# Experts' rows added to the residual in DRAM, in a two-layer decoder trunk

## The chip, the cores and the metric

One core of one Trainium2 chip runs the whole program. The metric is the device time of one execution in microseconds (us).

## The reference

Two layers work on x of 512 tokens by 1024. Each has a token mixer (RWKV-7 in the first, attention with a forget gate in the second), a layer norm, a mixture of 16 experts of which each token takes two, and another layer norm. The part that matters here, for each layer:

```
h   = layer_norm(ALPHA * h + mixed, ln_g[i, 0], ln_b[i, 0])
ffn = sum over the token's two experts of  gate * (silu(h @ w_gate) * (h @ w_up)) @ w_down
h   = layer_norm(ALPHA * h + ffn, ln_g[i, 1], ln_b[i, 1])      # LN_EPS 1e-5, ALPHA = sqrt(2)
```

The gates of a token's two experts are scores divided by their sum. With these inputs the experts of the first layer get, in the order in which the kernel takes them, 167, 82, 19, 59, 131, 65, 53, 4, 145, 53, 50, 6, 89, 62, 26 and 13 rows (1,024 in all); the second layer's counts differ by at most 9.

## The kernel before

Matmuls keep fp32 precision by splitting each operand in a high and a low part (`split`: ACT copies, DVE subtracts) and summing three products (`mm3`). The weights of an expert are six halves of 1 MB; SP loads them into a ring of eight buffers (`load`, `place`), and a buffer's next load is issued as soon as its half is split.

`After.norm` ends the first norm of a layer: tile i (128 tokens) is written to `hd` in DRAM, by POOL's queue, and by SP's for the last tile. `moe` then ranks the tokens, writes a table of slots to DRAM with scatters (L426) and reads it back as `TB`: for each expert's rows the token (`src`), a place in `yd` (`dst`: the token's row in the first or second 512 rows) and the gate.

The loop over experts (last lines of `moe`) issues, in this order: `more(e)`, which runs only where an expert has more than 128 rows (3 experts a layer) and scatters up to 64 rows of a second block; the gather of the first 128 rows of expert e+2 into `xg` (L251); `gather2(e+1)`, the rows past 128 of expert e+1 in halves, into `xo` (L259; it runs for every expert); and `expert(e)`. That multiplies, transposes the next expert's `xg` and, late, its `xo` (`xposeB`, L305), and ends with the scatter of 128 rows of `y` into `yd` (L334). Rows past an expert's count have an index out of range and are dropped. Scatters, gathers and their waits stand in order on POOL's queue. The scatters are declared independent of each other, since each slot of `yd` is written once. `rest` (over 192 rows) does not run with these inputs.

`Combine` adds the parts and takes the second norm. `load_h` brings h from `hd` during the last experts; `load_y` loads, after the last scatter, the two halves of `yd` for each of four tiles (eight loads of 512 KB on SP). The letter in `how` says who adds: D is DVE alone, V is PE with ALPHA h and one part and DVE with the other, P is PE alone, G is POOL and DVE. The layer norm follows (`ln_steps`), whose four passes with g and b go to DVE or POOL, whichever a planner (`Threads`) expects to be free sooner. In the first layer this stands at the head of `fox`: each normed tile is transposed and split, and the value projection (`t_values`, 24 matmuls per tile and half) starts on it; `FX_SCHED` holds the planner's start times of the four tiles (`TK`) and of the value weights (`TV`). In the second layer it ends the program, and each tile is stored.

Of the kernel before, what the change touches and what calls it, by code (L numbers as in the profile page):

```python
# [118 lines left out]

def ln_stats(C, z, n):  # L120
# [4 lines left out]
    nc.vector.tensor_scalar(sm[:,14:15],sm[:,13:14],LN_EPS,None,op0=ALU.add)  # L125
    nc.scalar.activation(sm[:,15:16],sm[:,14:15],AF.Sqrt)
# [50 lines left out]

def moe(C, L, W, hd, load, tail, late=()):

# [3 lines left out]
    with ExitStack() as ctx:  # L183
        p1=ctx.enter_context(tc.tile_pool(name=f"m{L}p1",bufs=1)); wk=ctx.enter_context(tc.tile_pool(name=f"m{L}k",bufs=1))
        fx=lambda n,shape,dt=F32: wk.tile(shape,dt,name=n,bufs=1)
        yd=C.dram.tile([1024,D],F32,name=f"yd{L}"); tab=C.dram.tile([8192,4],I32,name=f"tab{L}")
        TB=p1.tile([128,64,4],I32,name="TB"); TB2=p1.tile([128,64,4],I32,name="TB2")
# [84 lines left out]
        def slot(m): return his[m%NH],los[m%NH]  # L272
        src=lambda e,b=0: TB[:,4*e+b,0:1]; dst=lambda e,b=0: TB[:,4*e+b,1:2]; gate=lambda e,b=0: TB[:,4*e+b,2:3].bitcast(F32); gate2=lambda e,b=0: TB2[:,4*e+b,2:3].bitcast(F32)
        def xposeT(xg,hf,bk):
# [54 lines left out]
        def outB(n,y):  # L329
            t=(xo,su)[n][0:64]; p=(pgo,py[0])[n]  # L330
            nc.scalar.activation(t,p[64:128],AF.Copy); V.tensor_tensor(y[0:64,n*512:(n+1)*512],t,p[0:64],op=ALU.add)
        scat=[]
        def scatter(ix,y,n):
            st=nc.gpsimd.indirect_dma_start(out=yd[:,:],out_offset=bass.IndirectOffsetOnAxis(ap=ix[0:n],axis=0),  # L334
                in_=y[0:n],in_offset=None,bounds_check=2*T-1,oob_is_err=False)
            for o in scat: tc.declare_no_dep(st.ins,o.ins,reason="rows of other slots")
            scat.append(st)
        def more(e):

            y=ys[1-e%2 if e else 0]; w=[slot(6*e+j) for j in range(6)]; f2=gate2(e,1) if e else g0[:,1:2]  # L340
            with tc.If(rs[e]>128):
                guB(w[0],0); guB(w[1],1); nc.scalar.activation(xo,pgo,AF.Copy)
                if e==0: gates0(1)
                guB(w[2],2); upB(0,f2)
                guB(w[3],3); upB(1,f2); hidBT(0); hidBS(0); hidBT(1); hidBS(1)
                for n in range(2): dnB(w[4],4,n)
                for n in range(2): dnB(w[5],5,n); outB(n,y)
                scatter(dst(e,1),y,64)


        def expert(e):
# [16 lines left out]
            if next_: xposeB()  # L368
            lo(4); dnA(w[5],5,1); outA(1,y,fo); scatter(dst(e),y,128); hi(5); lo(5)
        def again(e,j):  # L370
            r=raws[6+j%2]; w=slot(6*e+j); place(r,L,W,6*e+j,nc.gpsimd); split(C,*w,r); return w
        def rest(e,blk):

            f=gate(e,blk); ix=dst(e,blk)
            if blk==1: V.memset(i2[0:64],int(BIG)); V.tensor_copy(i2[64:128],ix[64:128]); ix=i2
# [33 lines left out]
        V.tensor_reduce(red[:,1,:,None],ct(mt),axis=AX.X,op=ALU.add)  # L409
        V.tensor_tensor(red[:,2,0:4],red[:,1,0:4],red[:,1,4:8],op=ALU.add); V.reciprocal(red[:,2,0:4],red[:,2,0:4])  # L410
        V.tensor_tensor(C.rec[:,:,2].rearrange("p (c t) -> p c t",c=2).bitcast(F32),red[:,1].rearrange("p (c t) -> p c t",c=2),red[:,2:3,0:4].to_broadcast([128,2,NT]),op=ALU.mult)
# [33 lines left out]
        for e in range(NE):  # L445
# [4 lines left out]
            expert(e)  # L450
    return yd

class Combine:


    def __init__(s, C, hd, g, b):
        s.C,s.hd,s.g,s.b=C,hd,g,b; s.how='PPPP'
        s.h=[part(C.raws[4+i//2],i%2) for i in range(NT)]; s.y0=[part(C.raws[6+i//2],i%2) for i in range(NT)]
        s.gb,s.bb=part(C.raws[2],0),part(C.raws[2],1)
# [9 lines left out]
    def spread2(s):  # L469
        C=s.C  # L470
        for n in range(4): C.nc.scalar.activation(C.raws[2][:,n*512:(n+1)*512],C.bk[4+n],AF.Copy)
    def load_h(s, j):
        s.C.nc.sync.dma_start(s.C.raws[4+j].rearrange("p (i n) -> p i n",i=2),s.hd[j*256:(j+1)*256,:].rearrange("(i p) n -> p i n",p=128))
    def load_y(s, yd, y1, late):

        nc=s.C.nc; d=nc.sync.dma_start; s.y1=y1
        for i in range(NT):
            d(s.y0[i],yd[i*128:(i+1)*128,:]); d(y1[i],yd[T+i*128:T+(i+1)*128,:])
        if late: s.spread(); s.spread2()
        pe=[i for i in range(NT) if s.how[i] in 'PV']  # L480
        for i in pe: nc.scalar.activation(s.h[i],s.h[i],AF.Copy,scale=ALPHA); s.add(i,s.h[i],start=True,stop=False)
        for i in pe:
            s.add(i,s.y0[i],start=False,stop=s.how[i]=='V')
            if s.how[i]=='P': s.add(i,y1[i],start=False,stop=True)
    def add(s, i, t, **k):
        for n in range(2): s.C.nc.tensor.matmul(s.C.bk[2*i+n],s.C.ident,t[:,n*512:(n+1)*512],skip_group_check=True,**k)
    def steps(s, i, th):

        C=s.C; V=C.nc.vector; h,y0,y1,how=s.h[i],s.y0[i],s.y1[i],s.how[i]; z=C.bk[2*i:2*i+2] if how=='P' else h
        if how=='G':  # L490
            C.nc.gpsimd.tensor_tensor(y0,y0,y1,op=ALU.add); yield 'G',2.4,.1
            V.scalar_tensor_tensor(h,h,ALPHA,y0,op0=ALU.mult,op1=ALU.add); yield 'V',1.35
        elif how=='V':
            for n in range(2): N=slice(n*512,(n+1)*512); V.tensor_tensor(h[:,N],y1[:,N],C.bk[2*i+n],op=ALU.add)
            yield 'V',1.2
        elif how=='D':
            V.scalar_tensor_tensor(h,h,ALPHA,y0,op0=ALU.mult,op1=ALU.add); V.tensor_tensor(h,h,y1,op=ALU.add); yield 'V',2.55
        yield from ln_steps(C,th,z,i,s.h[i],s.gb,s.bb)

# [831 lines left out]
def trunk(nc, tc, a, out):  # L1331
    with ExitStack() as ctx:
        C=mk_common(nc,tc,ctx); moe_consts(C)
        nc.scalar.dma_start(C.rwt,a["router_w"].rearrange("(k p) e -> p k e",p=128)); nc.scalar.dma_start(C.rbt,bcast_row(a["router_bias"]))
        hd=[C.dram.tile([T,D],F32,name=f"hd{n}") for n in range(2)]
        lg=lambda n: (a["ln_g"][n//2,n%2],a["ln_b"][n//2,n%2])
# [16 lines left out]
        cb=[Combine(C,hd[n],*lg(2*n+1)) for n in range(2)]
        yd=moe(C,0,W,hd[0],load[0],2,(6,7))
        cb[0].how='DVPG'
        fox(C,cb[0],yd,F,AfterFox(C,hd[1],load[1],*lg(2)))
        yd=moe(C,1,W,hd[1],load[1],0)
# [33 lines left out]
```

## Time and profile before

| what | value |
|---|---|
| runs | 1673.84, 1676.75, 1679.83 us (median 1676.75) |
| profiled execution | 1676.42 us, its span 1674.7 us |
| busy: PE, DVE, ACT, POOL | 1486.3, 1172.9, 926.9, 517.1 us (89%, 70%, 55%, 31%) |
| moved by the DMA engines | 317.77 MB |

The shares are means over stages that are bound by different things: the experts run from about 560 to 905 us and from 1300 to 1640, the two combines from about 905 to 940 and from 1640 to the end.

### The profile page before, as it was taken

The page shows a single profiled execution, that of the slowest core. Times are in us where ns is not written, and L with a number is a line of the kernel's source. Part 1 is how long each engine was busy: PE and PEld are TensorE (multiplying, and loading weights), DVE is VectorE, ACT ScalarE, POOL GpSimd, SP SyncE. Part 2 cuts the span into 40 slices and gives each one's busy share as a digit, 9 for nine tenths or more (in the row PEclk, how much of TensorE's full clock was granted, in tenths as well). Part 3 has the DMA queues.
Part 4 walks back from the last instruction along what each step waited for, and adds up shares of the span by engine and source line. Part 5 has one row for each costly group of instructions (what it writes and reads, how often), then busy time and mean ns, then how long its engine had stood idle before and what let it go on. Part 6 is the DMA issues. An engine that isn't in the chain of part 4 may idle for free. (4 is left out here: it accounts for less than half of the span.)

```text
span 1674.7 us, 25018 instructions
## 1 busy us (share of the span) xinstructions
PE 1486.3 (89%) x9185; PEld 1202.8 (72%) x9185; DVE 1172.9 (70%) x1883; ACT 926.9 (55%) x1361; POOL 517.1 (31%) x423
## 2 busy tenths in 40 slices
PE   6998976989984799999999799999973999999995
PEld 2587765977763688888886677777763788888883
DVE  7547769576785497877996637556545696869984
ACT  2543764534334386867885446555333686858863
POOL 4104776313331333322431422111013232413421
PEclk8998997788986899999999899999985999999998
DMA  7326532033515598897994323112433697979963
GB/s 216 120 82 217 155 97 69 13 121 95 172 68 178 185 340 297 300 350 251 353 353 169 102 82 113 63 36 75 151 107 134 227 370 237 362 243 353 350 235 152
DMA packets 203605, 317.77 MB, mean 190 GB/s; under 512 B 27978, under 2 KB 123554, under 8 KB 203444
## 3 DMA queue, kind: packets, MB, share of 16 engines
q1 hardware_dynamic: 181060, 276.13, 48.4%
q0 software_dynamic: 17664, 33.11, 5.8%
q10 hardware_dynamic: 4720, 6.44, 1.1%
q8 instruction: 93, 1.52, 0.4%
q14 instruction: 68, 0.56, 0.1%
HBM read 304.80 MB, written 37.55 MB: 204 GB/s over the span
## 5 line engine op out<-in xcount | busy, mean ns | idle before, releaser
L202 DVE TENSOR_TENSOR wl<-raw,wh 128x2048 fp32r<-128x2048 f32 (+1 forms) x168 | 334.5, 2005 | 16.9 <-DMA tab<-rec,idx 6.5
L199 ACT ACTIVATE wh<-raw 128x2048 fp32r<-128x2048 f32 (+1 forms) x168 | 282.6, 1688 | 13.3 <-ACT wh L199 8.7
L68 PE MATMUL bank<-wh,xm 128*128 128x256 f32 (+1 forms) x768 | 250.2, 326 | 3.9
L69 PE MATMUL bank<-wl,xm 128*128 128x256 f32 (+1 forms) x768 | 245.4, 320 | 0.0
L70 PE MATMUL bank<-wh,xm 128*128 128x256 f32 (+1 forms) x768 | 245.2, 319 | 0.0
L334 POOL DMA_INDIRECT yd<-yt,TB x38 | 91.5, 2407 | 447.8 <-ACT yt L301 387.5
L68 PEld LDWEIGHTS bank<-wh,xm 128*128 128x128 f32 x768 | 144.7, 188 | 26.1 <-issue 14.6
L69 PEld LDWEIGHTS bank<-wl,xm 128*128 128x128 f32 x768 | 144.8, 189 | 11.4
L70 PEld LDWEIGHTS bank<-wh,xm 128*128 128x128 f32 x768 | 144.7, 188 | 11.3
L202 DVE TENSOR_TENSOR wl<-rawo,wh 128x2048 fp32r<-128x2048 f32 (+1 forms) x56 | 110.2, 1980 | 20.6 <-ACT wh L199 20.1
L68 PE MATMUL bank<-wh,wh 128*128 128x512 f32 x256 | 112.7, 440 | 3.1 <-DVE wl L1082 1.7
L68 PE MATMUL bank<-wh,hm 128*128 128x512 f32 x256 | 111.3, 435 | 2.9 <-ACT hm L64 2.9
L70 PE MATMUL bank<-wh,wl 128*128 128x512 f32 x256 | 102.1, 399 | 2.8 <-DVE wl L1268 2.8
L69 PE MATMUL bank<-wl,wh 128*128 128x512 f32 x256 | 101.5, 397 | 0.0
L70 PE MATMUL bank<-wh,hm 128*128 128x512 f32 x256 | 101.4, 396 | 0.0
L69 PE MATMUL bank<-wl,hm 128*128 128x512 f32 x256 | 100.9, 394 | 0.0
L199 ACT ACTIVATE wh<-rawo 128x2048 fp32r<-128x2048 f32 (+1 forms) x56 | 93.4, 1668 | 12.8 <-PE bank L70 9.0
L1090 POOL TENSOR_TENSOR wl<-raw,wh 128x512 fp32r<-128x512 f32 x29 | 40.8, 1418 | 87.7 <-ACT wh L1089 87.7
L259 POOL DMA_INDIRECT xo<-hd,TB x30 | 61.9, 2063 | 13.0 <-issue 8.0
L65 DVE TENSOR_TENSOR xm<-bank,xm 128x512 fp32r<-128x512 f32 x64 | 44.3, 692 | 29.8 <-ACT xm L64 26.9
L64 ACT ACTIVATE xm<-bank 128x512 fp32r<-128x512 f32 x64 | 38.3, 598 | 47.7 <-PE bank L275 38.8
L68 PEld LDWEIGHTS bank<-wh,wh 128*128 128x128 f32 x256 | 49.6, 194 | 16.4 <-issue 5.6
(545 smaller groups left out, 3557.7 us busy)
## 6 DMA issues: line engine op xcount, KB each, us to landing
raw<-in_moe_w_gate_dram SPq DMA_DIRECT2D x48, 1024.0 KB, 8.4
raw<-in_moe_w_up_dram SPq DMA_DIRECT2D x48, 1024.0 KB, 9.9
raw<-in_moe_w_down_dram SPq DMA_DIRECT2D x48, 1024.0 KB, 7.1
rawo<-in_moe_w_up_dram SPq DMA_DIRECT2D x16, 1024.0 KB, 5.6
rawo<-in_moe_w_down_dram SPq DMA_DIRECT2D x16, 1024.0 KB, 7.8
rawo<-in_moe_w_gate_dram SPq DMA_DIRECT2D x14, 1024.0 KB, 8.9
raw<-in_fx_w_in_dram SPq DMA_DIRECT2D x12, 1024.0 KB, 6.6
raw<-in_rw_wk_dram SPq DMA_DIRECT2D x4, 1024.0 KB, 12.4
```

Source lines behind the costliest of these rows:

```text
L64: nc.scalar.activation(hi,src,AF.Copy)
L65: nc.vector.tensor_tensor(lo,src,hi.bitcast(F32),op=ALU.subtract)
L68: nc.tensor.matmul(out,ah,bh,start=start,stop=False)
L69: nc.tensor.matmul(out,ah,bl,start=False,stop=False)
L70: nc.tensor.matmul(out,al,bh,start=False,stop=stop)
L199: Q=slice(None) if q is None else QS[q]; nc.scalar.activation(his[m%NH][:,Q],raws[m%NR][:,Q],AF.Copy)
L202: Q=slice(None) if q is None else QS[q]; V.tensor_tensor(los[m%NH][:,Q],raws[m%NR][:,Q],his[m%NH][:,Q].bitcast(F32),op=ALU.subtract)
L259: nc.gpsimd.indirect_dma_start(out=xo,out_offset=None,in_=hd.rearrange("t (h n) -> (t h) n",h=2), in_offset=bass.IndirectOffsetOnAxis(ap=T ...
L334: st=nc.gpsimd.indirect_dma_start(out=yd[:,:],out_offset=bass.IndirectOffsetOnAxis(ap=ix[0:n],axis=0), in_=y[0:n],in_offset=None,bounds_ch ...
L1090: (V if d else G).tensor_tensor(lo[n][:,Q],raw[:,Q],hi[n][:,Q].bitcast(F32),op=ALU.subtract)
```

## The change

The residual lives in a second DRAM tensor `zd`. `After.norm` writes each normed tile to it as well (on POOL's queue). The experts' scatters no longer put rows into `yd` but add them to `zd` at the token's row, with an accumulating indirect DMA. They are no longer declared independent: each waits for the one before. To make this a plain sum, the gates are divided by ALPHA (one more DVE operation on 128x4 in the routing), so that zd holds h + ffn/ALPHA, and the norm's epsilon is divided by ALPHA squared. `Combine` loads the four tiles of `zd` after the last scatter and norms them; `load_h`, `load_y`, the adds on PE, DVE and POOL and the letters go away. The planner's start times in `FX_SCHED` and at the end are moved (2, 5, 8, 11 and 20 become 0, 2, 4, 6 and 15; 3.0 i becomes 2.0 i).

```diff
 def moe
-        yd=C.dram.tile([1024,D],F32,name=f"yd{L}"); tab=C.dram.tile([8192,4],I32,name=f"tab{L}")
+        tab=C.dram.tile([8192,4],I32,name=f"tab{L}")
...
-        scat=[]
         def scatter(ix,y,n):
-            st=nc.gpsimd.indirect_dma_start(out=yd[:,:],out_offset=bass.IndirectOffsetOnAxis(ap=ix[0:n],axis=0),
-                in_=y[0:n],in_offset=None,bounds_check=2*T-1,oob_is_err=False)
-            for o in scat: tc.declare_no_dep(st.ins,o.ins,reason="rows of other slots")
-            scat.append(st)
+            nc.gpsimd.indirect_dma_start(out=zd[:,:],out_offset=bass.IndirectOffsetOnAxis(ap=ix[0:n],axis=0),
+                in_=y[0:n],in_offset=None,bounds_check=T-1,oob_is_err=False,compute_op=ALU.add)
...
-                scatter(dst(e,1),y,64)
+                scatter(src(e,1),y,64)
...
-            lo(4); dnA(w[5],5,1); outA(1,y,fo); scatter(dst(e),y,128); hi(5); lo(5)
+            lo(4); dnA(w[5],5,1); outA(1,y,fo); scatter(src(e),y,128); hi(5); lo(5)
...
-        V.tensor_tensor(red[:,2,0:4],red[:,1,0:4],red[:,1,4:8],op=ALU.add); V.reciprocal(red[:,2,0:4],red[:,2,0:4])
+        V.tensor_tensor(red[:,2,0:4],red[:,1,0:4],red[:,1,4:8],op=ALU.add); V.reciprocal(red[:,2,0:4],red[:,2,0:4]); V.tensor_scalar(red[:,2,0:4],red[:,2,0:4],1.0/ALPHA,None,op0=ALU.mult)
...
 class Combine
-    def load_h(s, j):
...
-    def load_y(s, yd, y1, late):
...
-    def add(s, i, t, **k):
...
+    def load_z(s):
+        for i in range(NT): s.C.nc.sync.dma_start(s.h[i],s.zd[i*128:(i+1)*128,:])
     def steps(s, i, th):
...
-        yield from ln_steps(C,th,z,i,s.h[i],s.gb,s.bb)
+        yield from ln_steps(s.C,th,s.h[i],i,s.h[i],s.gb,s.bb,eps=LN_EPS/ALPHA**2)
...
-FX_SCHED=(0,.5,-1,0,2,5,8,11,20)+(0,)*16
+FX_SCHED=(0,.5,-1,0,0,2,4,6,15)+(0,)*16
...
 def fox
-    comb.load_y(yd,[tp.tile([128,D],F32,name=f"y1{i}") for i in range(NT)],True)
+    comb.load_z(); comb.spread(); comb.spread2()
...
 class After
         (s.C.nc.sync if i==NT-1 else s.C.nc.gpsimd).dma_start(s.hd[i*128:(i+1)*128,:],out)
+        s.C.nc.gpsimd.dma_start(s.zd[i*128:(i+1)*128,:],out)
...
 def trunk
-            if k in (4,5): cb[0].load_h(k-4)
...
-        cb[1].how='PVPV'; cb[1].load_y(yd,[part(C.raws[i//2],i%2) for i in range(NT)],False)
+        cb[1].load_z()
...
-            yield 3.0*i
+            yield 2.0*i
```

## Rows read from the trace of the kernel before

**Rows 1.** The head of the profile page.
```profile
span 1674.7 us, 25018 instructions
```

**Rows 2.** Windows by stage: length, busy us per engine (count), PE clock, DMA share, GB/s.
```profile
905.00:935.00 30.00, 19.43 (x44) 8.98 (x42) 20.25 (x31) 11.49 (x18) 10.99 (x10) 0.74 0.71 249
...
1548.00:1568.00 20.00, 19.85 (x119) 17.07 (x118) 18.16 (x16) 16.38 (x17) 7.95 (x4) 1.00 1.01 359
```

**Rows 3.** POOL timeline, second layer's experts: start, us, operation, [idle before <-releaser].
```profile
1385.89 2.79 POOL L334 DMA_INDIRECT yd<-yt,TB  x1 [11.44 <-ACT yt L301]
1400.40 0.92 POOL L334 DMA_INDIRECT yd<-yt,TB  x1 [11.72 <-DVE yt L331]
...
1528.61 2.80 POOL L334 DMA_INDIRECT yd<-yt,TB  x1 [11.44 <-ACT yt L301]
...
1533.91 2.23 POOL L259 DMA_INDIRECT xo<-hd,TB  x1 [0.31 <-issue]
1547.59 2.80 POOL L334 DMA_INDIRECT yd<-yt,TB  x1 [11.45 <-ACT yt L301]
...
1552.89 2.23 POOL L259 DMA_INDIRECT xo<-hd,TB  x1 [0.31 <-issue]
...
1640.35 1.00 POOL L334 DMA_INDIRECT yd<-yt,TB  x1 [14.04 <-ACT yt L301]
```

**Rows 4.** DMA issues, us to landing: whole run; then at 1476, 1509, 1533.9, 1552.9.
```profile
raw<-in_moe_w_up_dram SPq DMA_DIRECT2D x48, 1024.0 KB, 9.9
...
yd<-yt,TB POOLq DMA_INDIRECT x1, 8.4
...
yd<-yt,TB POOLq DMA_INDIRECT x1, 9.4
...
xo<-hd,TB POOLq DMA_INDIRECT x1, 7.2
...
xo<-hd,TB POOLq DMA_INDIRECT x1, 8.5
```

**Rows 5.** PE timeline: the transposes of xo (L305).
```profile
1543.75 0.60 PE L305 MATMUL bank<-ident,xo 128*128 128x128 f32 x4
...
1562.73 0.60 PE L305 MATMUL bank<-ident,xo 128*128 128x128 f32 x4
```

**Rows 6.** Timeline of the middle combine, then ACT's in what follows.
```profile
908.33 0.34 SPq L478 DMA_DIRECT2D rawo<-yd  x1
...
912.07 1.23 DVE L497 SCALAR_TENSOR_TENSOR raw<-raw,rawo 128x1024 f32<-128x1024 f32 x1 [10.66 <-DMA rawo<-yd]
...
917.79 1.38 DVE L494 TENSOR_TENSOR raw<-y,bank 128x512 f32<-128x512 f32 x2
...
930.76 2.29 DVE L492 SCALAR_TENSOR_TENSOR raw<-raw,rawo 128x1024 f32<-128x1024 f32 x1
...
935.38 0.80 PE L68 MATMUL bank<-wh,wh 128*128 128x512 f32 x1 [1.66 <-DVE wl L1082]
...
960.86 1.28 ACT L1118 ACTIVATE rawo<-bank 128x512 f32<-128x512 f32 x2 [9.60 <-PE bank L70]
```

**Rows 7.** Timeline of the end.
```profile
1643.06 0.33 SPq L478 DMA_DIRECT2D rawo<-yd  x1
...
1650.81 0.70 DVE L123 BATCH_NORM_STATS2 sm<-bank 128x6 f32<-128x512 f32 x1 [14.68 <-PE bank L486]
...
1666.98 4.07 DVE L148 TENSOR_TENSOR raw<-raw,raw 128x512 f32<-128x512 f32 x6
```

**Rows 8.** Timeline of DVE, then ACT: last tile of a norm.
```profile
1242.32 1.28 DVE L123 BATCH_NORM_STATS2 sm<-raw 128x6 f32<-128x512 f32 x2
...
1248.23 0.60 ACT L155 ACTIVATE hT<-bank 128x512 f32<-128x512 f32 x1 [2.01 <-PE bank L154]
```

**Rows 9.** Timeline of ACT, then DVE: routing of the second layer.
```profile
1272.63 0.60 ACT L64 ACTIVATE xm<-bank 128x512 fp32r<-128x512 f32 x1 [8.89 <-issue]
...
1282.89 0.17 DVE L411 TENSOR_TENSOR rec<-red 128x8 f32<-128x8 f32 x1
```

More of the change, by code (lines that the diff above doesn't have):

```diff
@@ L118, in halves, with ln_stats @@
 def halves(z): return z if isinstance(z,list) else [z[:,0:512],z[:,512:1024]]
-def ln_stats(C, z, n):
+def ln_stats(C, z, n, eps=LN_EPS):
     nc=C.nc; sm=C.sm[:,n%4]
@@ L124, in ln_stats @@
     nc.vector.bn_aggr(sm[:,12:14],sm[:,0:12].rearrange("p (a b) -> p a b",a=2))
-    nc.vector.tensor_scalar(sm[:,14:15],sm[:,13:14],LN_EPS,None,op0=ALU.add)
+    nc.vector.tensor_scalar(sm[:,14:15],sm[:,13:14],eps,None,op0=ALU.add)
     nc.scalar.activation(sm[:,15:16],sm[:,14:15],AF.Sqrt)
@@ L138, in ln_affine, with ln_steps @@
     C.nc.vector.tensor_tensor(z,z,gb,op=ALU.mult); eng.tensor_tensor(z,z,bb,op=ALU.add)
-def ln_steps(C, th, z, i, out, gb, bb, mark=lambda n: None):
-    ln_stats(C,z,i); yield 'V',1.4,'S',.2,.1
+def ln_steps(C, th, z, i, out, gb, bb, mark=lambda n: None, eps=LN_EPS):
+    ln_stats(C,z,i,eps); yield 'V',1.4,'S',.2,.1
     ln_scale(C,i); yield 'V',.2,.1
@@ L175, in place, with moe @@
     queue.dma_start(raw.rearrange("p (k n) -> p k n",k=kk),(M[:,hf*n:(hf+1)*n] if w==1 else M[hf*128*kk:(hf+1)*128*kk,:]).rearrange("(k p) n -> p k n",p=128))
-def moe(C, L, W, hd, load, tail, late=()):
+def moe(C, L, W, hd, zd, load, tail, late=()):
     nc,tc=C.nc,C.tc; V=nc.vector
@@ L272, in slot @@
         def slot(m): return his[m%NH],los[m%NH]
[L273 removed]
+        src=lambda e,b=0: TB[:,4*e+b,0:1]; gate=lambda e,b=0: TB[:,4*e+b,2:3].bitcast(F32); gate2=lambda e,b=0: TB2[:,4*e+b,2:3].bitcast(F32)
         def xposeT(xg,hf,bk):
@@ L372, in rest @@
         def rest(e,blk):
-            f=gate(e,blk); ix=dst(e,blk)
+            f=gate(e,blk); ix=src(e,blk)
             if blk==1: V.memset(i2[0:64],int(BIG)); V.tensor_copy(i2[64:128],ix[64:128]); ix=i2
@@ L450, in moe, with __init__ @@
             expert(e)
-    return yd
 class Combine:
-    def __init__(s, C, hd, g, b):
-        s.C,s.hd,s.g,s.b=C,hd,g,b; s.how='PPPP'
-        s.h=[part(C.raws[4+i//2],i%2) for i in range(NT)]; s.y0=[part(C.raws[6+i//2],i%2) for i in range(NT)]
+    def __init__(s, C, zd, g, b):
+        s.C,s.zd,s.g,s.b=C,zd,g,b
+        s.h=[part(C.raws[4+i//2],i%2) for i in range(NT)]
         s.gb,s.bb=part(C.raws[2],0),part(C.raws[2],1)
@@ L471, in spread2 @@
         for n in range(4): C.nc.scalar.activation(C.raws[2][:,n*512:(n+1)*512],C.bk[4+n],AF.Copy)
-    def load_h(s, j):
-        s.C.nc.sync.dma_start(s.C.raws[4+j].rearrange("p (i n) -> p i n",i=2),s.hd[j*256:(j+1)*256,:].rearrange("(i p) n -> p i n",p=128))
-    def load_y(s, yd, y1, late):
[L476 to L484, printed above, removed]
-    def add(s, i, t, **k):
-        for n in range(2): s.C.nc.tensor.matmul(s.C.bk[2*i+n],s.C.ident,t[:,n*512:(n+1)*512],skip_group_check=True,**k)
-    def steps(s, i, th):
[L489 to L497, printed above, removed]
-        yield from ln_steps(C,th,z,i,s.h[i],s.gb,s.bb)
+    def load_z(s):
+        for i in range(NT): s.C.nc.sync.dma_start(s.h[i],s.zd[i*128:(i+1)*128,:])
+    def steps(s, i, th):
+        yield from ln_steps(s.C,th,s.h[i],i,s.h[i],s.gb,s.bb,eps=LN_EPS/ALPHA**2)
 def moe_consts(C):
@@ L1042, in fox_vload, with fox @@
     C.nc.sync.dma_start(k4(dst),P['win'][k*512:(k+1)*512,2048+n*512:2048+(n+1)*512].rearrange("(k p) n -> p k n",p=128))
-FX_SCHED=(0,.5,-1,0,2,5,8,11,20)+(0,)*16
-def fox(C, comb, yd, P, after):
+FX_SCHED=(0,.5,-1,0,0,2,4,6,15)+(0,)*16
+def fox(C, comb, P, after):
     nc,tc=C.nc,C.tc
@@ L1299, with __init__ @@
 class After:
-    def __init__(s, C, hd, load, gb, bb):
-        s.C,s.hd,s.load,s.gb,s.bb=C,hd,load,gb,bb
+    def __init__(s, C, hd, zd, load, gb, bb):
+        s.C,s.hd,s.zd,s.load,s.gb,s.bb=C,hd,zd,load,gb,bb
     def free(s, n): s.load(n)
@@ L1318, with __init__ @@
 class AfterFox(After):
-    def __init__(s, C, hd, load, lg, lb):
-        After.__init__(s,C,hd,load,part(C.raws[2],0),part(C.raws[2],1)); s.lg,s.lb=lg,lb
+    def __init__(s, C, hd, zd, load, lg, lb):
+        After.__init__(s,C,hd,zd,load,part(C.raws[2],0),part(C.raws[2],1)); s.lg,s.lb=lg,lb
     def free(s, n):
@@ L1334, in trunk @@
         nc.scalar.dma_start(C.rwt,a["router_w"].rearrange("(k p) e -> p k e",p=128)); nc.scalar.dma_start(C.rbt,bcast_row(a["router_bias"]))
-        hd=[C.dram.tile([T,D],F32,name=f"hd{n}") for n in range(2)]
+        hd,zd=[[C.dram.tile([T,D],F32,name=f"{c}d{n}") for n in range(2)] for c in "hz"]
         lg=lambda n: (a["ln_g"][n//2,n%2],a["ln_b"][n//2,n%2])
@@ L1344, in tail0 @@
             if k==3: cb[0].load_gb1()
-            if k in (4,5): cb[0].load_h(k-4)
         def tail1(k):
             if k==2: cb[1].load_gb()
-            if k in (4,5): cb[1].load_h(k-4)
         load=[loader(C,0,W,tail0),loader(C,1,W,tail1)]
         ctx.enter_context(tc.manual_schedule())
-        rwkv(C,a["x"][0],P,lambda gb,bb: After(C,hd[0],load[0],gb,bb),*lg(0))
+        rwkv(C,a["x"][0],P,lambda gb,bb: After(C,hd[0],zd[0],load[0],gb,bb),*lg(0))
         mk_ring(C)
[L1353 to L1357, printed above, removed]
-        cb[1].how='PVPV'; cb[1].load_y(yd,[part(C.raws[i//2],i%2) for i in range(NT)],False)
+        cb=[Combine(C,zd[n],*lg(2*n+1)) for n in range(2)]
+        moe(C,0,W,hd[0],zd[0],load[0],2,(6,7))
+        fox(C,cb[0],F,AfterFox(C,hd[1],zd[1],load[1],*lg(2)))
+        moe(C,1,W,hd[1],zd[1],load[1],0)
+        cb[1].load_z()
         th=Threads()
         def last(i):
-            yield 3.0*i
+            yield 2.0*i
             yield from cb[1].steps(i,th)
```

## The prediction

> **What bounds the kernel now.** I read the windows by stage first, then the POOL timeline of an expert stage, the landing of its DMAs, PE's waits there, and last the two stretches in which the combine runs.
>
> The span is 1674.7 us [rows 1]. The profiled run took 1676.42, so 1.7 lies around the span, and the median of the runs shown is 1676.75: all three agree within 0.1%. No single engine bounds it. In the expert stages PE is busy 19.85 of 20 us at a granted clock of 1.00 (2.4 GHz), with the DMA engines at a share of 1.01 and 359 GB/s: both are full, and nothing may be added to either lightly. In 905:935 PE has 19.4 busy us of 30 and most of that is not matmul of the model but the adding up of three parts; DVE has 20.3 [rows 2]. So there are three stretches to price: the expert stages, the combine in the middle, the combine at the end.
>
> In an expert stage POOL does for each expert: scatter, gather of 128 rows, gather of half rows into xo (called gather2). The reader is to see two distances. One scatter is issued 18.98 us after the one before (1528.61, 1547.59), or 14.51 where a second block's scatter comes between (1385.89, 1400.40) [rows 3]; a plain scatter lands 8.4 us after issue with 4 rows of valid data and 9.4 with 128 [rows 4]. And gather2, issued at 1533.91, lands 7.2 us later, at 1541.1, for a PE transpose that begins at 1543.75 without waiting: 2.6 us of slack [rows 3 to 5]. I worked this out for all 30: 4 that follow a second block's scatter have far more, the 26 others 1.3 to 3.4 us, with 2.5 in the middle; the tightest is gather2 at 1552.89, landed at 1561.4, used at 1562.73 [rows 3 to 5].
>
> **Removed in the middle combine.** Before: the first part is asked for at 908.33, and DVE, which waited for it, starts at 912.07 (3.7 us); DVE then spends 1.23 twice (L497), 1.38 (L494) and 2.29 (L492) on sums, 6.1 us, and the loads are eight instead of four. The first matmul of the value projection starts at 935.38, and its fourth unit of 24 matmuls is copied out at 960.86 [rows 6]. After: load_z is asked for when the last scatter has landed. The last scatter has 13 rows, issues in 1.00 us and landed in under 2.7 (1640.35 to the load at 1643.06, which waits for it) [rows 3, 7]. With the accumulate I give it 1.2 more, an estimate between 0 and a second such landing of 2.7. So the first tile is there at 908.3+1.2+3.7=913.3. From a tile's first statistics to the end of the copy of its first transposed half it took 6.5 us where little else ran (1242.32 to 1248.83) [rows 8]. So PE starts near 920, 15 us sooner. Can it be fed? DVE per tile: statistics and scales 2.0 (row 1.28, the rest small), four passes with g and b of which a third goes to POOL 1.8, two splits 1.4, each pass 0.69 as in L494: 5.2 us, against 24 matmuls of about 0.21, 5.1. Nearly even, so four units end near 920+21+2.5 (the granted clock is 0.74 in this stretch, a mean of its levels of 1.2 and 2.4 GHz [rows 2]) = 943.5, and the gain there is 17. I take 15 for the in-order queues. Bounds: 6 (only the DVE sums go, the start stays tied to something else) and 18. What comes after is PE work in a row, so the gain holds to the end of the stage.
>
> **Removed at the end.** First statistics at 1650.81 follow PE adds; the first load was asked for at 1643.06. After: 1643.06+1.2+3.7=1648.0, 2.8 sooner. DVE's two pairs of L494 go, 2.6 (the pair of the middle took 1.38 [rows 6]). DVE is the engine that runs through to 1671.05 (1666.98+4.07) [rows 7], so 5.4 us. Bounds: 2 (a last scatter 3 us later still) and 7.
>
> **Added, off the path.** Four writes of 512 KB to zd in each layer, on POOL's queue behind the four of hd, after each norm. POOL has nothing to do there, and gathers wait for hd alone, whose last write stays on SP. The tiles are overwritten by weight loads, which now also wait for the zd read. That delays the last of the first six weight halves by at most the 3.7 us in which 512 KB came in at 908.33 [rows 6], and it is hidden: ACT, which splits it, then stands idle 8.89 us until the gather is there [rows 9]. Without that cover it would cost up to 3.7 us per layer. One more DVE operation on 128x4 in the routing, before the table scatters that everything waits for: 0.17 by its neighbour [rows 9], 0.4 in all. The reads of h (2 MB a layer) and of two parts (4 MB) become one read of 2 MB, and 2 MB are written, and the scatters read some 4 MB: traffic is about even, but those 4 MB move into the expert stage.
>
> **Added, in the expert stage.** Each scatter now waits for the one before. With landings of 9.4 against 14.51 and 18.98 this wait is over before it is reached, as long as an accumulating scatter lands in about 14 us. Behind a late one stand the two gathers on POOL, and PE waits for xo. The dearer thing is x, what the accumulating scatter adds between its own issue and gather2's landing: a longer issue (2.80 now) plus the time its rows take in front of gather2's. From rows: 4 to 128 valid rows differ by 1.0 us in landing [rows 4], so doubling the traffic of some 50 rows (64 is the mean) adds about 0.5, and at four times the price 1.5. Issue: 0 more (as many rows), or double, 2.8. So x lies between 0 and 4.3; I take 1, nearest to the row that shows how little data matters. Cost is 26 times (x minus 2.5), if positive; at x=1 only the tightest use is touched at all: 0. Weight loads: 64 rows of 4 KB read once more at 359 GB/s [rows 2] are 0.7 us per expert. A load is asked for eight sixths of an expert ahead, 25 us, and lands in 9.9 [rows 4], so 15 us of delay are covered; it would take 20 experts in a row to use them up, and every second-block expert, 33 us for the same six loads, gives them back.
>
> The Trainium skill, DMA: Bandwidth & Descriptors, Rules for kernel authors, speaks against the change: nothing holds the bytes between the read and the write of an accumulating DMA, so each must wait for the earlier one's semaphore. By that rule and these rows the wait is there and costs nothing until a landing passes 14 us. The same page, Latency and other measured facts, gives HBM access 2 us at high load; as an estimate, one such read in front of the writes would make x 3 and the expert stages 13 us longer in all; no run here shows it yet.
>
> **Sum.** 1674.7 -15 -5.4 +0.4 +0 = 1654.7 in the span, with 1.7 around it 1656.4; against the median, 1657. About 0.3%, 5 us, is what a measurement can tell from no change.
>
> **The rivals.**
> *A, slower: the accumulating scatter is late for gather2.* One place, POOL's queue in front of xo, one price, 26 times (x-2.5). For it: 2.5 us is little, the DMA engines are full, issue is 2.80 where DVE runs beside and 1.00 where it does not [rows 3], so the issue is sensitive. Against: landing hardly knows the number of rows. Where a scatter issues twice as long and its rows cost four times, x=4.3, 47 us are lost and 20 won: 1703. It decides from x=3.3, where 26 times 0.8 eats the 20; at x=3.0 it is 1670. Chances: x over 3.5, 0.20 with C; 3.1 to 3.5 (no change, some 1677), 0.08; 2.5 to 3.1, 0.08.
> *B, the middle gain is mostly hidden.* If DVE's order, or the value weights that are loaded and split in the same stretch, holds PE, only the 6 us of sums come back, with 5.4 at the end: 1666. For it: DVE and PE per tile are almost even. Against: PE has no wait once it has begun. Chance 0.17.
> *C, the scatters chain.* If one takes over 19 us to land, POOL and with it each expert goes at its pace: at 22 us some 3 us times 26, 1735. It would be twice today's landing; inside the 0.20 of slower I give it 0.04.
>
> **Chances and range.** Forecast 0.47, B 0.17, A's mild part 0.08: faster 0.72. Same 0.08, slower 0.20. The likeliest case's own range is 1649 to 1664 (bounds 18 and 7, or 10 and 3). For 8 in 10 I reach from 1647 over B and the no-change case to 1684, which leaves A's upper part and C (0.15) and about 0.05 below.
>
> **What would show it.** Scatter issue near 2.8 and landing under 12; POOL waiting for ACT yt before each scatter, not for a scatter's DMA; no PE wait for xo at L305; scatters still 18.98 apart. The first value matmul about 10 us after the first z load is asked for (3.7 and 6.5), where it is 27 now. At the end DVE starting 5 us after that load and running on without sums. The prediction is wrong if scatters stand over 19 us apart, if PE waits for xo, or if the last scatter lands more than 3 us later than now.

## The result, and the profile after

The changed kernel took 1660.25 us in the median (9 runs) where the kernel before took 1675.49 (9 runs): a ratio of 0.9914, with a 95% interval of 0.9893 to 0.9934. That is 14 to 15 us faster, where 20 were forecast. The head of the page after, its busy row, the software queue, and the rows of the scatter and of gather2:

```profile
span 1658.4 us, 24906 instructions
...
PE 1457.0 (88%) x9125; PEld 1190.5 (72%) x9125; DVE 1165.6 (70%) x1873; ACT 921.7 (56%) x1357; POOL 526.8 (32%) x431
...
q0 software_dynamic: 18816, 37.31, 7.9%
...
L335 POOL DMA_INDIRECT zd<-yt,TB x38 | 113.7, 2991 | 444.5 <-ACT yt L302 382.5
...
L260 POOL DMA_INDIRECT xo<-hd,TB x30 | 61.8, 2060 | 11.8 <-issue 8.3
```

The span is 16.3 us shorter than in [rows 1]. To see where, I cut it at the first and last scatter of each layer. The part up to the first scatter varied between 570.3 and 579.5 us over the 14 kernels profiled, with or without the edits, so it says nothing here (578.2 before, 574.2 after). The other parts repeat within about 1 us, but for the first step of the experts and the middle of one kernel (both below), and are what I compare:

| stretch, us | before | after |
|---|---|---|
| experts, layer 1 (first to last scatter) | 327.47 | 329.19 |
| middle: last scatter of layer 1 to first of layer 2 | 407.25 | 398.68 |
| experts, layer 2 | 327.47 | 327.18 |
| end: last scatter to the end of the span | 34.35 | 29.13 |

The 1.7 us more in layer 1 lie between its first two scatters: 17.9 us apart after, 15.8 to 18.5 in the later profiles of the same expert code that hold nothing up on POOL. With the kernel before's experts this step takes 16.1 or 16.2, and once 17.4 (e2, layer 2). In layer 2 the steps of 17 us and more have a granted clock of 0.80 or 0.81, in layer 1, with nothing held up on POOL, of 1.00; what lengthens those, and whether the change makes them more frequent, is open. But for this one step, up to 2.4 us longer, the expert stages pay nothing; the middle gives 8.6 us and the end 5.2.

**Expert stage.** The POOL timeline of layer 2 after, against [rows 3]; then DMA issues with their us to landing (the scatter of 1536.51, the gather2 of 1541.83, the last scatters of the two layers), against [rows 4]; then PE's transposes of xo, against [rows 5]; then the two windows of [rows 2]:

```profile
1517.53 3.40 POOL L335 DMA_INDIRECT zd<-yt,TB  x1 [11.45 <-ACT yt L302]
...
1536.51 3.40 POOL L335 DMA_INDIRECT zd<-yt,TB  x1 [11.46 <-ACT yt L302]
1540.22 1.31 POOL L252 DMA_INDIRECT xg<-hd,TB  x1 [0.30 <-issue]
1541.83 2.21 POOL L260 DMA_INDIRECT xo<-hd,TB  x1 [0.31 <-issue]
...
1629.27 1.58 POOL L335 DMA_INDIRECT zd<-yt,TB  x1 [13.47 <-ACT yt L302]
```

```profile
zd<-yt,TB POOLq DMA_INDIRECT x1, 10.3
...
xo<-hd,TB POOLq DMA_INDIRECT x1, 7.5
...
zd<-yt,TB POOLq DMA_INDIRECT x1, 4.6
...
zd<-yt,TB POOLq DMA_INDIRECT x1, 4.2
```

```profile
1551.65 0.60 PE L306 MATMUL bank<-ident,xo 128*128 128x128 f32 x4
1570.63 0.60 PE L306 MATMUL bank<-ident,xo 128*128 128x128 f32 x4
```

```profile
905.00:935.00 30.00, 14.24 (x58) 10.21 (x56) 21.40 (x43) 15.85 (x28) 13.58 (x13) 0.60 0.65 214
1548.00:1568.00 20.00, 19.85 (x119) 17.10 (x118) 18.23 (x17) 16.37 (x19) 6.91 (x3) 1.00 1.03 343
```

The scatter issues in 3.40 us instead of 2.80 and lands in 10.3 instead of 9.1 (the scatter of the same expert before, at 1547.59; over the 30 that are neither a second block's nor a layer's last, the medians are 10.8 and 9.1). Still they stand 18.98 us apart, each waiting for ACT's yt and none for a scatter's DMA. The reader should see why PE notices nothing. DVE's splits of weights run beside POOL's issues; before (scatter at 1528.61), then after (scatter at 1536.51):

```profile
1528.23 4.48 DVE L202 TENSOR_TENSOR wl<-raw,wh 128x2048 fp32r<-128x2048 f32 x2
1531.71 1.89 POOL L251 DMA_INDIRECT xg<-hd,TB  x1 [0.30 <-issue]
...
1536.14 4.48 DVE L203 TENSOR_TENSOR wl<-rawo,wh 128x2048 fp32r<-128x2048 f32 x2
```

The gather of 128 rows starts 0.6 us later after the scatter than it did, but ends 0.9 us after the second of the two splits in both kernels (1533.60 and 1532.71; 1541.53 and 1540.62): it issues in 1.31 us instead of 1.89. So gather2 is issued 5.3 us after the scatter in both, and the longer issue is gone before it reaches gather2. That lands at 1549.3 for a transpose at 1551.65 that has no bracket, so no wait. Over the 26 tight cases the time from a scatter's issue to gather2's landing has a median of 12.88 us, 12.57 before: x, as the prediction called it, is 0.3. The windows show the stage as full as it was.

**Middle.** After the last scatter, issued at 903.41 (905.63 before, so subtract 2.2 from the times of [rows 6] to compare). First DVE, then PE, then ACT:

```profile
911.36 1.29 DVE L123 BATCH_NORM_STATS2 sm<-raw 128x6 f32<-128x512 f32 x2 [12.38 <-DMA raw<-zd]
...
917.73 2.24 PE L1055 MATMUL bank<-ident,raw 128*128 128x128 f32 x8 [11.80 <-DVE raw L148]
921.30 1.11 PE L1055 MATMUL bank<-ident,raw 128*128 128x128 f32 x4 [1.33 <-POOL raw L148]
924.90 3.46 PE L1055 MATMUL bank<-ident,raw 128*128 128x128 f32 x12 [2.48 <-DVE raw L148]
928.01 0.78 PE L68 MATMUL bank<-wh,wh 128*128 128x512 f32 x1
...
921.56 0.20 ACT L126 ACTIVATE sm<-sm 128x1 f32<-128x1 f32 x1 [2.02 <-DVE sm L125]
921.67 0.58 ACT L1056 ACTIVATE wh<-bank 128x512 fp32r<-128x512 f32 x1
922.15 2.92 ACT L135 ACTIVATE raw<-raw,sm 128x512 f32<-128x512 f32 x4
924.97 1.68 ACT L1056 ACTIVATE wh<-bank 128x512 fp32r<-128x512 f32 x3
...
951.29 1.28 ACT L1094 ACTIVATE rawo<-bank 128x512 f32<-128x512 f32 x2 [9.60 <-PE bank L70]
```

The sums are gone and the first tile is there at 911.36, 7.95 us after the last scatter. But the first half tile, transposed by PE from 917.73, is copied out only at 921.67, because ACT's queue holds the square roots of later tiles ahead of it (the one at 921.56 waits 2.02 us for DVE). And PE's queue has six half-tile transposes ahead of the first value matmul; the last three of them (twelve instructions) wait for DVE until 924.90. So the first value matmul starts at 928.01: 24.6 us after the last scatter, 29.75 before. The third and fourth units (one row) are copied out from 47.9 us after it, 55.2 before; the eighth 83.6, 90.3 before. Of the 2.2 us won between the first matmul and the fourth unit some 1.3 are the clock's, an estimate: the granted clock was 0.50 (1.2 GHz) for the first 4.6 us of the value matmuls before and for 2.1 after, then 1.00, and at 0.50 half of that time is lost.

**End**, against [rows 7], on DVE:

```profile
1637.04 1.29 DVE L123 BATCH_NORM_STATS2 sm<-raw 128x6 f32<-128x512 f32 x2 [11.99 <-DMA raw<-zd]
...
1647.77 6.70 DVE L148 TENSOR_TENSOR raw<-raw,raw 128x512 f32<-128x512 f32 x9
```

DVE starts 7.8 us after the last scatter (10.5 before) and runs on without sums to 1654.5.

### The profile page after: what moved, and what is told of

It reads as the page before. It is cut to its first block, busy times and chain, and to the rows that moved or that the text cites. A ratio compares the mean times of both kernels' runs of the same rounds, so it can differ in the third digit from the quotient of the medians.

```text
span 1658.4 us, 24906 instructions
## 1 busy us (share of the span) xinstructions
PE 1457.0 (88%) x9125; PEld 1190.5 (72%) x9125; DVE 1165.6 (70%) x1873; ACT 921.7 (56%) x1357; POOL 526.8 (32%) x431
## 5 line engine op out<-in xcount | busy, mean ns | idle before, releaser
L203 DVE TENSOR_TENSOR wl<-raw,wh 128x2048 fp32r<-128x2048 f32 (+1 forms) x168 | 334.4, 2004 | 18.6 <-DVEq L266 13.1
L335 POOL DMA_INDIRECT zd<-yt,TB x38 | 113.7, 2991 | 444.5 <-ACT yt L302 382.5
L203 DVE TENSOR_TENSOR wl<-rawo,wh 128x2048 fp32r<-128x2048 f32 (+1 forms) x56 | 110.2, 1979 | 21.8 <-ACT wh L200 21.3
L310 PE MATMUL bank<-wh,xh 128*128 128x256 f32 (+1 forms) x144 | 45.6, 344 | 18.3 <-ACTq L434 9.7
## 6 DMA issues: line engine op xcount, KB each, us to landing
rawo<-in_moe_w_gate_dram SPq DMA_DIRECT2D x14, 1024.0 KB, 11.9
```

Of the source, the lines that this page charges most:

```text
L203: Q=slice(None) if q is None else QS[q]; V.tensor_tensor(los[m%NH][:,Q],raws[m%NR][:,Q],his[m%NH][:,Q].bitcast(F32),op=ALU.subtract)
L310: nc.tensor.matmul(out,x,h,start=start,stop=False); nc.tensor.matmul(out,x,l,start=False,stop=stop)
L335: nc.gpsimd.indirect_dma_start(out=zd[:,:],out_offset=bass.IndirectOffsetOnAxis(ap=ix[0:n],axis=0), in_=y[0:n],in_offset=None,bounds_check ...
```

## The experiments

All twelve, each timed beside the kernel before. "Middle" and "end" are the stretches of the table above, from the one profiled execution.

| kernel | median us | ratio to before, 95% interval | middle | end |
|---|---|---|---|---|
| changed kernel | 1660.25 | 0.9914 (0.9893 to 0.9934) | 398.7 | 29.1 |
| e1, only layer 2 changed | 1668.19 | 0.9961 (0.9942 to 0.9980) | 404.2 | 29.6 |
| e2, only layer 1 changed | 1669.02 | 0.9962 (0.9945 to 0.9978) | 398.5 | 35.2 |
| e3, values planned 5 us sooner | 1671.43 | 0.9973 (0.9959 to 0.9987) | 407.0 | 29.5 |
| e4, before with chained scatters | 1675.12 | 1.0011 (0.9991 to 1.0031) | 406.8 | 34.4 |
| e5, scatters overwrite | 1643.89 | 0.9813 (0.9790 to 0.9837) | 396.6 | 27.8 |
| e6, gather2 held up by 9 memsets | 1674.32 | 0.9987 (0.9966 to 1.0008) | 399.6 | 29.7 |
| e7, gather2 held up by 20 memsets | 1697.60 | 1.0139 (1.0110 to 1.0167) | 399.6 | 29.8 |
| e8, tiles written twice more | 1663.11 | 0.9926 (0.9905 to 0.9947) | 399.0 | 29.6 |
| e10, changed, old start times | 1669.28 | 0.9971 (0.9949 to 0.9994) | 408.3 | 29.8 |
| e11, values planned 2 us sooner | 1668.96 | 0.9965 (0.9944 to 0.9987) | 404.1 | 29.8 |
| e12, splits planned 3 us sooner | 1663.70 | 0.9929 (0.9907 to 0.9952) | 397.3 | 29.7 |
| e13, before with the new start times | 1688.27 | 1.0090 (1.0063 to 1.0116) | 422.4 | 33.5 |

**One layer at a time (e1, e2).** Each keeps the old scatters, sums and start times in the other layer:

```diff
-        cb=[Combine(C,zd[n],*lg(2*n+1)) for n in range(2)]
+        cb=[OldCombine(C,hd[0],*lg(1)),Combine(C,zd[1],*lg(3))]   (e1)
+        cb=[Combine(C,zd[0],*lg(1)),OldCombine(C,hd[1],*lg(3))]   (e2)
```

> Only the second layer adds into DRAM; the first layer keeps its parts, its combine and its start times. The sum of the prediction says the end is worth 5.4 us: 0.9968 of the kernel before. The rival reading, that the end gains nothing by itself and that all 16 us come from the middle, says 1.000. In the trace DVE should start about 5 us before the place it has in the kernel before, counted from the last scatter's issue.

> Only the first layer adds into DRAM; the second keeps its parts. The prediction's sum puts 15 us here: 0.991. What the trace of the changed kernel shows (units of the value projection 7.4 us sooner, counted from the last scatter of the first layer) says 0.9955. If this run and the one with the second layer alone add up to the whole, nothing is shared between the two ends.

Each gives some 6.5 us of the median. e2's middle is 8.8 us shorter than before and e1's end 4.7: the forecast's 15 for the middle was too much, its 5.4 for the end was near. e1's middle is 3 us shorter though its combine there is the old one: 2.1 of them are there at the eighth unit (88.2 us after the last scatter, 90.3 before). The granted clock was 0.91 and 0.83 in its first two stretches of 20 us, where the kernel before had 0.83 and 0.66, so the clock alone can move a middle by some 2 us.

**The values first (e3).** The prediction's PE start assumed nothing of the later tiles in front of the value matmuls. A lead of 5 us in the planner puts four value matmul groups behind the first two transposes:

```diff
-FX_SCHED=(0,.5,-1,0,0,2,4,6,15)+(0,)*16
+FX_SCHED=(0,.5,-1,0,0,2,4,6,15,5)+(0,)*15
```

> The changed kernel, with the value projection of the first half emitted 5 planner us sooner, so that PE's queue holds the first tile's matmuls ahead of the transposes of tiles 2 and 3. Theory one: what the prediction missed in the middle is the order of PE's queue (six transposes before the first matmul); then the first matmul starts near 923 instead of 928 and the kernel gains 4 to 6 us, 0.988 of the kernel before. Theory two: DVE, which norms and splits the tiles, sets the pace; then it stays at 0.9914.

First a row of e3's PE timeline, then its windows of 10 us (last scatter at 901.90), then two windows of 20 us of the changed kernel (last scatter at 903.41):

```profile
921.89 0.80 PE L68 MATMUL bank<-wh,wh 128*128 128x512 f32 x1 [3.44 <-DVE wl L1058]
...
940.00:950.00 10.00, 7.94 (x35) 6.22 (x34) 2.58 (x4) 2.75 (x5) 1.27 (x1) 1.00 0.00 0
...
960.00:970.00 10.00, 7.83 (x37) 6.16 (x36) 4.31 (x14) 4.31 (x7) 1.29 (x1) 1.00 0.48 149
...
990.00:1000.00 10.00, 7.90 (x36) 6.22 (x34) 4.20 (x7) 7.12 (x13) 2.58 (x2) 1.00 0.17 46
...
943.41:963.41 20.00, 20.00 (x90) 16.28 (x89) 0.09 (x1) 2.44 (x5) 0.00 (x0) 1.00 0.00 0
...
983.41:1003.41 20.00, 20.00 (x93) 16.01 (x91) 12.94 (x23) 13.12 (x25) 7.35 (x7) 1.00 0.46 147
```

The transposes were indeed in the way: the first matmul now starts 20.0 us after the last scatter, 4.6 sooner. But the middle is 8.3 us longer than in the changed kernel. PE, which is fully busy in the changed kernel's like stretches, waits 2 us in each of three windows. Part of the early start is also only an exchange: the four half-tile transposes that no longer stand before the first matmul are done between the later ones. So an early start is not a gain kept, and neither of my theories had that.

**The chain's wait (e4).** The kernel before, with the declaration removed that keeps its scatters from waiting for each other:

```diff
-            for o in scat: tc.declare_no_dep(st.ins,o.ins,reason="rows of other slots")
```

> The kernel before, with its plain scatters no longer declared independent, so that each waits for the one before. The prediction says the wait is over before it is reached (9.4 us of landing against 14.5 and 19.0): no change, within 0.3%. Rival C, that a chain of scatters sets the pace, would show scatters more than 18.98 us apart and over 0.5% more time.

1.0011 (0.9991 to 1.0031), expert stages of 327.6 and 327.5: the wait costs nothing. The Trainium skill, DMA: Bandwidth & Descriptors, Rules for kernel authors, asks for such a wait with accumulating DMAs; in the changed kernel, which has it, no landing takes over 11.9 us and no scatter comes less than 14.5 after the one before.

**The price of the add (e5).** `compute_op=ALU.add` is left out; nothing else changes.

> The changed kernel with the 38 scatters writing their rows instead of adding them; the chain, the gathers and the one-sum combine stay. It leaves out the addition to the residual, so its data differ (its experts' rows stand alone in zd). It prices the accumulate itself. By the trace of the changed kernel: the landing of the last scatter of each layer goes back from 4.2 to 4.7 us to the 2.6 to 2.7 of the kernel before, so each combine starts 1.5 to 2 us earlier; the scatter's issue goes back from 3.4 us to 2.8 beside a busy VectorE, with nothing to win in the expert stages, where 2.3 us of slack remain: 1656 to 1658 us, 3 to 4 us under the changed kernel (ratio to the kernel before 0.988 to 0.990). Rival (the add is free at the ends too, and the later landing comes from the longer issue on GpSimd or from something else): the landings stay above 4 us and the time stays at 1660. Rival two (the add also slows the 26 chained gathers): over 8 us under the changed kernel.

The time is 16 us under the changed kernel, but most of that is no price: with other data the second layer's routing is another, and one expert fewer needs a second block (37 scatters, and a 14.5 us step gone from layer 2's experts). Rows of e5: the page's scatter row, then POOL after the last scatter of layer 1, then DVE's first statistics:

```profile
L335 POOL DMA_INDIRECT zd<-yt,TB x37 | 90.7, 2451 | 433.1 <-ACT yt L302 383.6
...
907.01 1.00 POOL L335 DMA_INDIRECT zd<-yt,TB  x1 [13.95 <-ACT yt L302]
909.88 0.20 POOL L1038 MEMSET mneg<- 128x128 bf16 x1 [1.88 <-DMA zd<-yt,TB]
...
913.13 1.29 DVE L123 BATCH_NORM_STATS2 sm<-raw 128x6 f32<-128x512 f32 x2 [10.36 <-DMA raw<-zd]
```

Statistics start 6.1 us after the scatter's issue, against 7.95 with the add; the middle is 2.1 us shorter and the end 1.3. Layer 1's experts, whose data are the same, keep their 19.0 us steps. So the add costs some 3.4 us in all, at the two ends, as the first theory had it, and nothing among the experts.

**The slack (e6, e7).** POOL is held up between the two gathers:

```diff
+            for _ in range(9): nc.gpsimd.memset(scr,0.0)      (20 in e7)
             if e+1<NE: gather2(e+1)
```

> The changed kernel with GpSimd held up by 9 small memsets between the scatter and the second gather of each expert, an estimated 1.6 to 2 us each time, to test the slack on which the expert-stage term rested (the rival that a later scatter delays the second gather). The trace of the changed kernel has a median of 2.3 us and a least of 1.2 us between the landing of the second gather and TensorE's need. By that the delay is mostly swallowed: 0 to 8 us in all over some 26 delayed gathers, 1660 to 1668 us. If the slack were not there (the delay lands on TensorE in full), 26 times 1.8 us is 47 us: near 1707.

> The same with 20 memsets, an estimated 3.6 to 4.2 us each time. By the slack of 2.3 us, 26 times (3.9 - 2.3) is about 42 us: 1690 to 1715 us, with TensorE's waits for the second gather's tile in the chain. If the expert stage had much more slack (the next expert can start on other rows, or the wait is made up within the expert), the time stays under 1675; if none, 26 times 3.9 is 101 us: near 1760.

The group of PE's xo transposes (busy, mean ns, then idle before them with releasers): the changed kernel, e6, e7.

```profile
L306 PE MATMUL bank<-ident,xo 128*128 128x128 f32 x128 | 20.1, 282 | 8.2 <-DMA xo<-hd,i 8.2
```

```profile
L306 PE MATMUL bank<-ident,xo 128*128 128x128 f32 x128 | 21.0, 289 | 17.1 <-DMA xo<-hd,i 9.4 <-DMA xo<-hd,TB 7.6
```

```profile
L306 PE MATMUL bank<-ident,xo 128*128 128x128 f32 x128 | 21.8, 295 | 36.1 <-DMA xo<-hd,TB 26.9 <-DMA xo<-hd,i 9.2
```

Nine memsets of 0.216 us are 1.9 us, 20 are 4.2; gather2's own issue gets 0.2 and 0.8 us shorter, so it comes some 1.7 and 3.4 us later. PE's waits for xo by gather2 go from nothing to 7.6 and 26.9 us. The second is 26 times (3.4-2.3) = 29, so the rival's formula held; the first is more than a median would say, since the tightest slacks are 1.2. e6's median lies 14 us above the changed kernel's (12 by the two ratios), beyond what I had expected (0 to 8). Of the 13.4 us between the two profiled executions 9.2 are in the expert stages, 1.5 in the middle and the end, and 2.7 before the first scatter, where kernels differ by as much without a reason.

**The writes (e8).** One more write of each normed tile, to its own buffer, on POOL's queue:

```diff
+        s.C.nc.gpsimd.dma_start(s.C.zz[i*128:(i+1)*128,:],out)
```

> The changed kernel with a second write of each normed tile (512 KB) to a buffer of its own in DRAM, beside the write to zd that the change put on GpSimd's queue. The forecast costed the new writes at nothing, since the tiles follow each other by more than a write takes and the first scatter comes later: so no change, 1659 to 1662 us. Rival (the writes or their issue on GpSimd delay the first experts' gathers): each write adds its issue of about 1 us and some 3 us of transfer on the last tile of each layer, 4 to 8 us in all: 1664 to 1668.

0.9926 (0.9905 to 0.9947) beside 0.9914, and a middle of 399.0 beside 398.7: the writes cost nothing that can be measured. The intervals would still hide 3 us, and the median stands 2.9 higher, between the two theories; the middle, where one set of writes lies, decides for none.

**The start times (e10 to e13).** The change also moved the planner's start times, which I had priced inside the combine's terms.

```diff
-FX_SCHED=(0,.5,-1,0,0,2,4,6,15)+(0,)*16
+FX_SCHED=(0,.5,-1,0,2,5,8,11,20)+(0,)*16       (e10; also 3.0*i for 2.0*i in the last combine)
+FX_SCHED=(0,.5,-1,0,0,2,4,6,15,2)+(0,)*15      (e11)
+FX_SCHED=(0,.5,-1,0,0,2,4,6,12)+(0,)*16        (e12)
```

> The changed kernel with the planner's start times of the kernel before (tiles of the middle at 2, 5, 8, 11 and splits at 20; tiles of the last combine 3 apart). The retiming is part of the change, and I costed it inside the combine's term. If the time is won by the later tiles' transposes standing behind the first matmuls, the old times, which put them so less, would be as good: 1658 to 1662 us. If the retiming is what turns the missing sums into time, it costs 3 to 6 us: 1663 to 1667.

> The changed kernel with a lead of 2 us of planned time for the first half of the value matmuls, so that four transposes of the later tiles, not six, are queued before the first pair of value matmuls. It is the mild form of the lead of 5 that moved the first matmul 4.6 us earlier and lost 8 us later to waits within the interleaved queue. If what was lost came from interleaving itself, this lies between: 1664 to 1668 us. If there is an order with both, this one keeps some 2 us of the earlier start and loses nothing: 1657 to 1659.

> The changed kernel with the splits of the value weights planned 3 us sooner (12 in place of 15), which also lets two value matmul groups in ahead of two of the transposes. If the first value matmul waits for the splits or the transposes queued ahead of it, it starts 2 to 3 us sooner and the time falls to 1657 to 1659 us. If ScalarE's and GpSimd's order for the four tiles sets the middle (the splits then push the tiles' square roots and scalings back), it is slower: 1662 to 1668.

e13 is the kernel before with its two lines of start times replaced by those of the changed kernel.

> The kernel before with nothing of the change but the planner's new start times (tiles of the middle at 0, 2, 4, 6 and splits at 15; tiles of the last combine 2 apart). The changed kernel with the old times gained only 5 to 6 us of the 15. If the retiming is a gain of its own, which the kernel before could have had too, this is about 9 us under the kernel before: near 1666 (0.9945). If the new times pay only where the sums are gone (in the kernel before VectorE and GpSimd still make sums between the tiles' normings, so tiles that are planned closer only wait for each other), it lies between 1672 and 1680 (0.998 to 1.003), and the two parts of the change are worth more together than singly.

This is the main finding. In the middle, by the two parts of the change:

| middle, us | old start times | new start times |
|---|---|---|
| three parts summed | 407.3 (before) | 422.4 (e13) |
| one sum loaded | 408.3 (e10) | 398.7 (changed) |

Three profiles have the sums and times of the first cell: 407.3, 406.8 (e4) and 404.2 (e1). With the old times, loading one sum is worth nothing in the middle; with the sums still made, the new times cost 15 us. Together they win 8.6. At the end the two parts nearly add up: 4.6 by the one sum (e10), 0.9 by the times (e13), 5.2 together. In e10 the start is as good as in the changed kernel: the first value matmul comes 24.2 us after the last scatter, the eighth unit after 82.8. What it won is lost far behind. PE's waits in e10 (last scatter at 901.66):

```profile
993.61 0.80 PE L68 MATMUL bank<-wh,wh 128*128 128x512 f32 x1 [2.59 <-DVE qs L1164]
...
1163.58 0.50 PE L68 MATMUL bank<-wh,wh 128*128 128x512 f32 x1 [2.06 <-ACT wh L1243]
1168.91 0.79 PE L70 MATMUL bank<-wh,wl 128*128 128x512 f32 x1 [1.72 <-DVE wl L1244]
1172.73 0.47 PE L1187 MATMUL bank<-kh,qs 128*128 128x128 f32 x1 [1.59 <-DVE st L1197]
```

In the changed kernel PE has only one wait over 1.5 us after the first value matmul in the first 300 us of the stretch:

```profile
1165.91 0.80 PE L70 MATMUL bank<-wh,wl 128*128 128x512 f32 x1 [2.21 <-DVE wl L1244]
```

So 2.6 us are lost 92 us into the stretch and 3.2 more some 260 us into it. e10's rows show waits of 5.8 us more, of the 9.6 by which its middle is longer. Behind them the granted clock stands at 0.50, for longer than in the changed kernel; two windows of e10, then one of the changed kernel:

```profile
993.60:996.90 3.30, 3.29 (x8) 2.64 (x9) 3.23 (x4) 0.24 (x1) 1.16 (x1) 0.50 0.91 308
1164.20:1177.70 13.50, 9.90 (x27) 6.45 (x27) 9.77 (x19) 8.66 (x20) 7.10 (x5) 0.50 0.24 89
...
1165.70:1172.40 6.70, 6.07 (x17) 4.48 (x18) 6.29 (x17) 3.38 (x10) 1.29 (x1) 0.50 0.49 161
```

Half of PE's busy time at this level is lost, 6.6 us against 3.0, so at most 3.6 more, an estimate. Like operations of ACT and DVE come (in the median) some 4 us later than in the changed kernel 100 us into the stretch and 7.9 later at 300 us, which waits and clock together account for; the last 1.7 us come behind that, at the first gathers of the second layer's experts. e10 moves the tiles' and the splits' times back together, so which of the two does it is open. In e13 the loss starts at once: POOL's sum of one tile (L491) and its passes stand in one queue, and PE waits for them. POOL, then PE (last scatter at 900.37):

```profile
917.42 2.34 POOL L491 TENSOR_TENSOR rawo<-rawo,y 128x1024 f32<-128x1024 f32 x1 [13.37 <-DMA y<-yd]
...
920.70 1.87 POOL L148 TENSOR_TENSOR raw<-raw,raw 128x512 f32<-128x512 f32 x1 [0.94 <-ACT raw L135]
...
926.53 2.82 PE L1079 MATMUL bank<-ident,raw 128*128 128x128 f32 x12 [9.39 <-POOL raw L148]
...
936.26 0.79 PE L68 MATMUL bank<-wh,wh 128*128 128x512 f32 x1 [0.62 <-DVE wl L1082]
```

Its first value matmul comes 35.9 us after the last scatter, 6.1 later than before. The rest of its 15 us comes behind, as in e10: at 997.75 PE has waited 3.84 us, at 1176.90 to 1186.06 three times, 5.4 in all (2.2 before), both times with the clock at 0.50 behind. I had expected e13 between 1672 and 1680; it was slower still, so the sense was right and the size not. e11 is another order that starts well (22.3 us after the last scatter) and loses later (404.1). e12 starts its values 20.2 us after the last scatter, 4.4 sooner, has the eighth unit 3.4 sooner and keeps 1.4 of it at the stage's end (397.3); its median is not lower, with 2.7 us more in the first steps of its expert stages and intervals that overlap. So the first theory had the sooner start right and the time not; the second's range holds the median, but the middle is not longer, on which it rests. Whether this order is better is open. No kernel here that adds the experts to the residual was faster than the changed one.

## Why the prediction was right, and where it was not

- **Sign and kind: right.** Both combines got shorter and the experts did not get longer.
- **Expert stage, 0: right.** x was put at 1 and is 0.3. One sign failed, "Scatter issue near 2.8": it rose by 0.6 us, to 3.40. I had counted a longer issue into x in full; it does not reach gather2, which is issued 5.3 us after the scatter as before, and x is all landing. Rival A is a real mechanism with the price given (e7), but the change doesn't reach it. Of the Trainium skill, DMA: Bandwidth & Descriptors, Latency and other measured facts, I had made an estimate of x = 3 and 13 us; the trace does not agree, at 0.3 and no wait of PE.
- **Chain wait, 0: right**, shown by e4. Rival C falls with landings of at most 11.9 us.
- **Writes to zd and the routing operation:** the writes are free as far as e8 can tell; the 0.4 us of the routing operation was not measured by itself.
- **End, 5.4: right**, 5.2 in the span, 4.7 in e1. The last landing rose by 1.5 to 2 us and not 1.2; e5 puts that on the add.
- **Middle, 15: wrong in size**, 8.6. The step that failed is "So PE starts near 920, 15 us sooner". It took 6.5 us from a tile's first statistics to its copied half, measured where one tile ran alone [rows 8]; here it took 10.9, since ACT and PE took the work of four interleaved tiles in the order in which it was queued, and PE began the values at 928.0, which is 930.2 in the times of [rows 6]: 5.2 us sooner, not 15. The sign in the profile that I had named, the first value matmul 10 us after the load of z, was 19.9. The feeding was priced well: from the first matmul to the copy of the fourth unit 23.3 us, forecast 23.5.
- **"What comes after is PE work in a row, so the gain holds to the end of the stage": wrong as a rule.** e10 had 7.5 us at the eighth unit and none at the stage's end; e3 had 4.6 us more at the first matmul and lost 8.3. That the changed kernel kept its gain is owed to the new start times, which I did not price as a part of their own.
- **Luck in the total.** The forecast, 1657, lies 3 us from the median; rival B (1666: only the sums come back) lies 6 off on the other side. But of the 20.4 us of its two terms the stretches show 13.8, and B's 6 for the middle is nearer to 8.6 than my 15 is. B's reason came true in part, since PE waits for DVE's order before its first value matmul. In the profiled execution 3.9 of the 16.3 us lie before the first scatter, where the change was not shown to do anything. The range given for the likeliest case was also summed wrongly: bounds of 18 and 7 make 1652, not 1649.

## What to carry to other kernels

When work at the head of a stage is removed and the order of the rest is written out by a planner, price the removal and the new order as two parts: here neither won in the middle alone, and the pair won 8.6 us. A latency measured on a lone tile is a lower bound where several tiles share the queues; count what stands ahead in each queue. Look at the granted clock behind each wait of PE, too: in e10 it cost up to 3.6 us beside 5.8 of waits. An accumulating scatter may be priced by three numbers, its issue, its landing when the engines are full, and the landing of the last one, for here only the last had somebody waiting for it.

## What the runs showed of the hardware that was not expected

- When DVE runs a split of weights (L202, in the changed kernel L203) as POOL begins to issue an indirect DMA, the issue ends a fixed time after that split: 0.9 us for the plain scatter (all 30 such) and the gathers of both kernels, 1.5 for the scatter with the add (all 30). Where DVE idles, the issue itself takes 0.9 to 1.1 us, with the add 1.4 to 1.6. So the add makes an issue some 0.5 to 0.6 us longer, and most of the 2.80 or 3.40 us is the time until DVE's split is done.
- A last scatter of few rows lands in 4.2 to 4.6 us with the add and 2.6 without, while in the full expert stage the median goes from 9.1 to 10.8.
- The 128-row gather behind the scatter issued in 1.31 to 1.43 us on average in the kernels with the add in both layers, against 1.70 in the kernel before and 1.73 in e5, whose scatters are plain. By the fixed time above this is no faster gather: it starts later and ends behind the same split.
